# Five of 22 gate and value pairs of a gated MLP's up projection by seven quarter products, on one Trainium2 core

## Chip, cores and metric

One core of a Trainium2 chip runs the whole layer. The metric is device time in microseconds from the start to the end of one execution; lower is better. Engines are named as in the profile: PE (TensorE, with PEld for its weight loads), DVE (VectorE), ACT (ScalarE), POOL (GpSimd), and SP, whose queue issues most DMAs.

## What is computed

One layer of a streaming encoder on 512 tokens of width 1024, all in float32: parallel token mixers, cross attention into 256 memory tokens, and a gated MLP. The change is in the MLP, which is the last stage:

```python
hf = _rms_norm(x, norm_ffn_pre[l])
u = _dwconv_causal(hf @ w_up[l], ffn_dw[l]) + ffn_dw_b[l]      # w_up: 1024 x 5632, kernel of 3 taps
u_g, u_v = jnp.split(u, 2, axis=-1)                           # 2816 channels each
yff = (jax.nn.silu(u_g) * u_v) @ w_down[l]                    # w_down: 2816 x 1024
x = x + _rms_norm(yff, norm_ffn_post[l])
```

## The kernel before, in words

**Products of three terms.** A float32 matrix is held as a high part rounded to the type that PE multiplies fast, and a low part, the rest. `mm3` (L239) makes a product of three matmuls: high by high, high by low, low by high. `split` (L152) and `split_weights` (L179) make the two parts: an ACT cast for the high one, a DVE subtraction for the low one (L190 and L191 for weights, L1612 and L1613 in the last product).

**The order of work.** `run_blocks` (L203) takes jobs from a generator. Each job names a block of weights, which is loaded and split three jobs ahead, and a body that issues its matmuls. Split weights go into four tiles of each part, used in turn (`weights_tile`, L145). Raw weights come through two tiles `wr`, by SP's queue. From the program order a scheduler lays out each engine's queue when the program is built, by its own estimate of when things are ready. On the chip each engine then works through its queue in that fixed order. PSUM's eight banks are four tags of two (`sc`, `tr`, `mm`, `av`).

**The up projection** (`up_jobs`, L1550). 2816 channels are 22 blocks of 128. Pair j is the gate block and the value block of the same channels; its two jobs are n = 2j and 2j + 1. A job's product has 8 slices of the inner dimension by 3 terms: 24 matmuls of 512 tokens into one bank. `done` (L1553) turns the bank into the convolved channels: one ACT instruction (L1557), two DVE taps (`taps`, L590, recorded at L594). After the value job the gate is formed with a tanh (L1561) and two DVE operations (L1562, L1564). The result is the left half of a tile `qa` or `qb` of the pair of blocks. The first four jobs are done in two halves of 256 tokens, since the last tokens of `hf` come late.

**The last product** (`down_jobs`, L1599) is already made of seven products in place of eight: the 2x2 blocks are channel blocks and tokens on one side, channel blocks and output columns on the other. It needs sums of the activations, which POOL makes (`activation_sums`, L564, four operations of 256 columns for each two pairs), and sums of `w_down`, which the class `Sums` (L527) loads on ACT's queue, makes on DVE (L542 to L545) and stores to DRAM during the up projection. They come back as `dw` tiles, a ring of four buffers. The residual stays in SBUF in `ns.out` until the end (`finish`, L1704).

**Ends.** `norm_task` (L1290) gives `hf`, tile by tile of 128 tokens, and writes the residual into `ns.out`. `open_ffn` (L1538) frees the tiles of the attention and opens those of the MLP.

Of the kernel before, what the change touches and what calls it, by code (L numbers as in the profile page):

```python
# [17 lines left out]
F32 = mybir.dt.float32  # L18
# [20 lines left out]
HALF_SHIFT = 16  # L39
BIG = -float(2.0 ** 100)  # L40
# [43 lines left out]
def hybrid_layer(ctx: ExitStack, tc: tile.TileContext, a: dict, out: bass.AP):  # L84
# [146 lines left out]
    def matmul(ps, lhs, rhs, start, stop):  # L231
        PE.matmul(ps, lhs, rhs, start=start, stop=stop)  # L232
        bg.clock += max(int(math.prod(rhs.shape[1:])), 256) * 0.00042
# [293 lines left out]
    class Sums:  # L527


        def __init__(self, w, pairs, tile, queue, name):  # L530
            self.w, self.tile, self.queue, self.held = w, tile, queue, {}
            self.pairs, self.dram = pairs, dram.tile([pairs * P, 2 * D], F32, name=name)
# [7 lines left out]
        def add(self, q):  # L540
            (b11, b12), (b21, b22) = ((x[:, :S], x[:, S:]) for x in self.held[q])
            V.tensor_tensor(b22, b22, b12, ALU.subtract)  # L542
            V.tensor_tensor(b12, b12, b11, ALU.subtract)
            V.tensor_tensor(b11, b22, b11, ALU.add)
            V.tensor_tensor(b21, b21, b11, ALU.subtract)  # L545
# [762 lines left out]
    def open_mix_out():  # L1308
        close(m2)
        ns.res_, resp = new_pool("res", False)  # L1310
        ns.xr, ns.normed = None, []
        ns.out = [resp.tile([P, D], F32, name=f"res{t}") for t in range(NT)]
# [191 lines left out]
    def open_cross_out():  # L1504
# [5 lines left out]
        ns.hf = new_ht()  # L1510

# [26 lines left out]
    def open_ffn():  # L1538
        bg.drain("n1")
        close(ns.work_)  # L1540
        close(ns.xp_)
        close(ns.xm_)
        ns.fp_, ns.fp = new_pool("ffn", False)
        ns.work = ns.fp
        ns.quart = [(ns.fp.tile([P, 4, S // 2], F32, tag=f"qa{q}", name="qa"),
                     ns.fp.tile([P, 3, S // 2], F32, tag=f"qb{q}", name="qb")) for q in range(NF // 2)]
        ns.post = ns.fp.tile([P, D], F32, name="g_ffn")
        G.dma_start(ns.post, a["norm_ffn_post"][0].partition_broadcast(P))

    def up_jobs():  # L1550
        st, held = {}, []

        def done(j, i, ps):  # L1553
            if i == 0:
                st[j] = ns.fp.tile([P, 2, S], F32, tag="c", name="c", bufs=2)
            c, ch = st[j], i * NF + j
            st["first"] = A.activation(c[:, i], ps, AF.Identity, bias=pc("fb", ch), scale=pc("fdw2", ch)).ins  # L1557
            st["taps"] = taps(c[:, i], ps, lambda k: pc("fdw01", k * 44 + ch), 3).ins
            if i == 1:
                th = ns.fp.tile([P, S], F32, tag="th", name="th")  # L1560
                A.activation(th, c[:, 0], AF.Tanh, scale=0.5)  # L1561
                V.scalar_tensor_tensor(th, th, 1.0, c[:, 0], ALU.add, ALU.mult)  # L1562
                x = ns.quart[j // 2]
                V.scalar_tensor_tensor(x[j % 2][:, 0:2].rearrange("p a b -> p (a b)"), th, 0.5, c[:, 1],  # L1564
                                       ALU.mult, ALU.mult)
                if j % 2:
                    activation_sums(*x, G)


        for n in range(2 * NF):  # L1570
            def body(hi, lo, n=n):
                j, i = divmod(n, 2)
                if n > 3:
                    ps = bank()
                    channel_major(ps, (hi, lo), ns.hf)
                    done(j, i, ps)

                    q = n // 3 - 2
                    if 0 <= q < NF // 2:
                        with tc.issue_after(st["taps" if n % 3 == 0 else "first"]):  # L1580
                            (ns.sums.add, ns.sums.store, ns.sums.load)[n % 3](q + 2 * (n % 3 == 2))
                    return
                if n == 0:
                    bg.drain("n0")
                ps = bank(("mm", "sc")[n % 2])
                (channel_major if n else by_pass)(ps, (hi, lo), ns.hf, slice(0, S // 2))
                held.append((j, i, ps, (hi, lo)))
                if n == 3:
                    open_ffn()
                    for j, i, ps, w in held:  # L1590
                        (channel_major if i or j else by_pass)(ps, w, ns.hf, slice(S // 2, S))
                        done(j, i, ps)
                    ns.sums = Sums(w_down, NF // 2, lambda: ns.fp.tile([P, D], F32, tag="dw", name="wp", bufs=4), A,
                                   "sums")
                    ns.sums.load(0)
                    ns.sums.load(1)
            yield *cols(w_up, n % 2 * DFF + n // 2 * P), body, V, same, HALF_SHIFT if n < 4 else 0

    def down_jobs():  # L1599
# [4 lines left out]
        def load(n):  # L1604
            while len(raws) < min(n, 2 * len(order)):
                (phase, q), job = order[len(raws) // 2], len(raws) % 2
                raw = ns.fp.tile([P, D], F32, tag="dw", name="dw", bufs=4)
# [3 lines left out]
        def split_to(hi, lo, x):  # L1611
            A.copy(hi, x)  # L1612
            V.tensor_tensor(lo, x, hi.bitcast(F32), ALU.subtract)  # L1613

        def activations(phase, q):
# [13 lines left out]
            split_to(hi, lo, ns.quart[q][phase].rearrange("p a b -> p (a b)"))  # L1629
# [3 lines left out]
        def weights(phase, q, job):  # L1633
# [5 lines left out]
            if (phase, job) == (1, 1):  # L1639
                both = ns.fp.tile([P, D], F32R, tag=f"qa{q}", name="n4")  # L1640
# [3 lines left out]
            if (phase, q) == (1, pairs - 1):  # L1644
                hi, lo = (ns.fp.tile([P, D], F32R, tag="dw", name="dwr", bufs=4) for _ in range(2))
# [15 lines left out]
        def square(x, i, pieces=1):  # L1661
            n, ms = S // pieces, []
            for c in range(pieces):
                ms.append(ns.fp.tile([P, 1], F32, tag=f"pm{i}", name=f"pm{i}", bufs=4))
                A.activation(ns.fp.tile([P, S], F32, tag="th", name="junk")[:, :n], x[:, c * n:(c + 1) * n], AF.Square,
# [6 lines left out]
        def middle(job):  # L1672
# [11 lines left out]
            z7 = parts["z7"] = ns.fp.tile([P, 2, S], F32, name="z7")  # L1684
# [29 lines left out]
        def ends():  # L1714
# [23 lines left out]
            spare = [ns.fp.tile([P, D], F32, tag="dw", name="o", bufs=4) for _ in range(2)]  # L1738
# [81 lines left out]
```

## Time and profile before

| | |
|---|---|
| three runs | 1055.25, 1055.68 (median), 1055.97 us |
| the profiled execution | 1055.79 us, of which the profile spans 1054.0 us |
| first to last instruction of the MLP stage | about 696 to 1054 us of the span |
| mean granted clock of TensorE | 0.997 |

The profile shows one execution. Its page gives busy time by engine, slices of the span, the chain of work that ended last and the costliest groups of instructions; views of the trace give busy time by stage, groups by line and shape, single instructions in order of time, and waits. A PE instruction's own duration in these views is longer than the distance to the next one's start, since matmuls are pipelined: for PE's pace the starts count.

### The profile page before, as it was taken

To read this page: it belongs to the slowest core of one execution; us is meant where nothing else is said; L and a number is where in the kernel's file an instruction comes from. 1 tells how busy PE (TensorE), PEld (TensorE's weight loads), DVE (VectorE), ACT (ScalarE), POOL (GpSimd) and SP (SyncE) were. 2 spreads that over 40 slices of the span, in tenths; PEclk is the share of its full clock that TensorE was granted. 3 is DMA by queue.
4 is the path that set the end of the run, shared out by engine and by line. 5 is a ranking of instruction groups with operands and counts; after the bars stand their busy time and mean duration, and the time that the engine had idled before them with its cause. 6 is when DMAs were issued, how large, how long until landed. Compare 5 with 4: busy or idle time off the path is not lost.

```text
span 1054.0 us, 14559 instructions
## 1 busy us (share of the span) xinstructions
PE 1041.7 (99%) x5295; PEld 886.8 (84%) x5295; DVE 807.1 (77%) x1280; ACT 501.9 (48%) x823; POOL 184.3 (17%) x309
## 2 busy tenths in 40 slices
PE   9999999999999999999999999999999999999996
PEld 8888888888888988888888899998888888888885
DVE  6899997668667467867487798777878777777795
ACT  5322222277465365655444566554333333355661
POOL 4000000300231233433011031121112111111001
PEclk9999999999999999999999999999999999999998
DMA  8854434742342353232359644135576676626662
GB/s 276 282 168 102 103 100 142 193 109 81 116 140 82 100 161 101 80 100 85 96 172 284 207 132 126 60 111 190 186 243 229 214 233 215 196 81 211 210 188 80
DMA packets 165373, 163.08 MB, mean 155 GB/s; under 512 B 6527, under 2 KB 136172, under 8 KB 165045
## 3 DMA queue, kind: packets, MB, share of 16 engines
q1 hardware_dynamic: 152995, 119.91, 38.0%
q0 software_dynamic: 5824, 19.03, 6.2%
q10 hardware_dynamic: 6482, 23.21, 5.7%
q8 instruction: 42, 0.69, 0.3%
q14 instruction: 30, 0.25, 0.1%
HBM read 139.03 MB, written 23.09 MB: 154 GB/s over the span
## 4 chain that ended last, share of the span: by engine, by line
PE 99%; DVE 0%; ACT 0%; issue 0%; POOL 0%; POOLq 0%; DVEq 0%; ACTq 0%
PE ps_mm L232 51%; PE ps_av L232 31%; PE ps_sc L232 8%; PE ps_tr L232 4%; PE ps_tr L236 2%; PE ps_mm L442 1%; PE ps_av L442 1%; PE ps_mm L384 0%; PE ps_sc L389 0%; DVE o L1710 0%; PE ps_tr L426 0%; POOL st_m L270 0%; POOLq L1816 0%; ACT hth L155 0%; ACT hth L432 0%
## 5 line engine op out<-in xcount | busy, mean ns | idle before, releaser
L190 ACT CAST wh<-wr 128x1024 fp32r<-128x1024 f32 (+1 forms) x142 | 148.8, 1049 | 273.3 <-PE ps_mm L232 175.0
L191 DVE TENSOR_TENSOR wl<-wr,wh 128x1024 fp32r<-128x1024 f32 (+1 forms) x142 | 178.5, 1258 | 79.0 <-ACT wh L190 78.8
L232 PE MATMUL ps_mm<-hth,wh 128*128 128x512 f32 (+1 forms) x592 | 221.1, 380 | 0.2 <-ACT hth L155 0.2
L232 PE MATMUL ps_mm<-htl,wh 128*128 128x512 f32 (+1 forms) x592 | 220.7, 379 | 0.0
L232 PE MATMUL ps_mm<-hth,wl 128*128 128x512 f32 (+1 forms) x592 | 220.6, 379 | 0.0
L232 PE MATMUL ps_av<-htl,wh 128*128 128x512 f32 (+1 forms) x352 | 131.8, 374 | 0.0
L232 PE MATMUL ps_av<-hth,wh 128*128 128x512 f32 (+1 forms) x352 | 131.8, 374 | 0.0
L232 PE MATMUL ps_av<-hth,wl 128*128 128x512 f32 (+1 forms) x352 | 131.6, 374 | 0.0
L232 PEld LDWEIGHTS ps_mm<-hth,wh 128*128 128x128 f32 x592 | 109.6, 188 | 20.4 <-ACT hth L155 0.8
L232 PEld LDWEIGHTS ps_mm<-hth,wl 128*128 128x128 f32 x592 | 109.5, 188 | 20.1
L232 PEld LDWEIGHTS ps_mm<-htl,wh 128*128 128x128 f32 x592 | 109.6, 188 | 19.7
L665 DVE SCALAR_TENSOR_TENSOR y<-y,par,y 128x482 f32<-128x482 f32 (+29 forms) x120 | 83.3, 735 | 0.1
L232 PEld LDWEIGHTS ps_av<-hth,wl 128*128 128x128 f32 x352 | 66.1, 188 | 11.9
L232 PEld LDWEIGHTS ps_av<-hth,wh 128*128 128x128 f32 x352 | 66.2, 188 | 11.8
L232 PEld LDWEIGHTS ps_av<-htl,wh 128*128 128x128 f32 x352 | 66.0, 188 | 11.7
L1613 DVE TENSOR_TENSOR wl<-dw,wh 128x1024 fp32r<-128x1024 f32 x32 | 40.2, 1262 | 13.3 <-ACT wh L1612 13.1
L1612 ACT CAST wh<-dw 128x1024 fp32r<-128x1024 f32 x32 | 33.4, 1051 | 23.4 <-PE ps_tr L232 7.9
L1058 POOL TENSOR_SCALAR fbias<-ck,cq 128x128 f32<-128x128 f32 (+3 forms) x32 | 28.2, 888 | 63.0 <-DVE st L1065 59.7
L1561 ACT ACTIVATE th<-c 128x512 f32<-128x512 f32 x22 | 13.9, 632 | 48.0 <-DVE c L594 48.0
L155 ACT CAST pth<-ps_tr 128x512 fp32r<-128x512 f32 (+3 forms) x56 | 23.5, 448 | 24.7 <-PE ps_tr L236 24.6
L594 DVE SCALAR_TENSOR_TENSOR c<-ps_mm,par,c 128x510 f32<-128x510 f32 (+1 forms) x44 | 32.8, 744 | 0.7
L156 DVE TENSOR_TENSOR ptl<-ps_tr,pth 128x512 fp32r<-128x512 f32 (+3 forms) x56 | 27.5, 512 | 5.9 <-ACT pth L155 5.4
(493 smaller groups left out, 2132.5 us busy)
## 6 DMA issues: line engine op xcount, KB each, us to landing
wr<-in_w_up SPq DMA_DIRECT2D x44, 512.0 KB
wr<-in_w_in SPq DMA_DIRECT2D x38, 512.0 KB
wr<-in_w_gate SPq DMA_DIRECT2D x32, 512.0 KB
wp<-in_w_down ACTq DMA_DIRECT2D x22, 512.0 KB
sums<-wp ACTq DMA_DIRECT2D x22, 512.0 KB
dw<-sums SPq DMA_DIRECT2D x44, 256.0 KB
wr<-in_w_branch SPq DMA_DIRECT2D x16, 512.0 KB
wide<-in_w_out SPq DMA_DIRECT2D x12, 512.0 KB
```

Of the source, the lines that this page charges most:

```text
L155: A.copy(hi, ps)
L156: V.tensor_tensor(lo, ps, hi.bitcast(F32), ALU.subtract)
L190: order(A.copy(hi, raw[:, :n]))
L191: low.tensor_tensor(lo, raw[:, :n], hi.bitcast(F32), ALU.subtract)
L232: PE.matmul(ps, lhs, rhs, start=start, stop=stop)
L236: PE.transpose(ps, x, ident[:n, :n])
L442: keep(PE.matmul(banks[c][:, :S // 2], w[p == 1][:, k, c * P:(c + 1) * P], ht[p == 2][:, i * 4 + k, :S // 2], start=(i, p, k) == (0, 0, 0) ...
L594: ins = V.scalar_tensor_tensor(dst[:, s:], src[:, :S - s], w(k), dst[:, s:], ALU.mult, ALU.add)
L665: ins = V.scalar_tensor_tensor(dst[:, s:], src[:, :S - s], pc("conv_dw", k * 4 + j), dst[:, s:], ALU.mult, ALU.add)
L1058: G.tensor_scalar(bias[:, :w], ck[j][:, :w], -1.0, cq[:, qt, head:head + 1], ALU.mult, ALU.add)
L1612: A.copy(hi, x)
L1613: V.tensor_tensor(lo, x, hi.bitcast(F32), ALU.subtract)
```

## The change

Five pairs, j = 4, 7, 10, 13 and 16, are computed as 2x2 blocks in Winograd's form of Strassen's scheme. The blocks of the weights are gate and value by the two halves of the inner dimension (A11, A12, A21, A22), those of `hf` the halves of the inner dimension by two halves of the tokens. Seven products of 4 slices by 3 terms of 256 tokens take the place of the pair's 48 matmuls of 512 tokens.

- POOL forms four sums of `hf` once, behind the first four jobs (`token_terms`, eight operations of 1024 columns); ACT and DVE split them into the tiles that held the residual. For that, each finished residual tile is stored to a DRAM tensor `kept` on SP's queue in `norm_task`, and loaded again (`reload`) in the last product's second half.
- For each of the five pairs DVE forms four sums of the weights, 512 columns each. Three and a half weight tiles are split, not two. The raw weights come into the ring `dw`, which gets seven buffers.
- The five jobs of such a pair (three with seven products' weights, two of the next pair, done in the plain way between them) interleave, so that a bank read by ACT or DVE is not written at once again.
- Silu replaces tanh and one DVE operation, for all pairs.
- The sums of `w_down` take one step in a pair of seven products and its partner, two steps in a plain pair, and four in each of the last four pairs (j = 18 to 21). POOL's sums of the activations all move to these last four pairs, 44 operations as before. Splits of activations in the last product are made in two instructions, not one.

The diff, cut to its core:

```diff
+SEVEN_AT = (4, 7, 10, 13, 16)
...
@@ norm_task
+        else:
+            SP.dma_start(ns.kept[t * P:(t + 1) * P, :], ns.out[t])
...
+    def ring(dtype=F32, name="dw"):
+        return ns.fp.tile([P, D], dtype, tag="dw", name=name, bufs=7)
...
+    def token_terms():
+        tok = [slice(i * S // 2, (i + 1) * S // 2) for i in range(2)]
+        b = {}
+        for k, t in ((0, 0), (0, 1), (1, 1), (1, 0)):
+            ks = slice(4 * k, 4 * k + 4)
+            x = b[k, t] = ring(name="b").rearrange("p (k c) -> p k c", k=4)
+            G.tensor_tensor(x, ns.hf[0][:, ks, tok[t]].bitcast(F32), ns.hf[1][:, ks, tok[t]].bitcast(F32), ALU.add)
+            if (k, t) == (0, 1):
+                G.tensor_tensor(b[0, 0], x, b[0, 0], ALU.subtract)
...
+        for i, n in ((0, (0, 0)), (1, (1, 1)), (2, (0, 1)), (3, (1, 0))):
+            split(b[n], *ns.terms[i])
...
+        def gated(c, j):
+            A.activation(c[:, 0], c[:, 0], AF.Silu)
+            V.tensor_tensor(ns.quart[j // 2][:, j % 2 * 2:j % 2 * 2 + 2].rearrange("p a b -> p (a b)"), c[:, 0],
+                            c[:, 1], ALU.mult)
...
+        def quart_sums(n):
...
+            for q in range(len(ns.quart_sums), n):
...
+                G.tensor_tensor(two[:, 0], x[:, 1], x[:, 3], ALU.add)
+                G.tensor_tensor(two[:, 1], x[:, 0], x[:, 1], ALU.subtract)
+                G.tensor_tensor(x[:, 1], two[:, 0], x[:, 0], ALU.subtract)
+                G.tensor_tensor(one, x[:, 2], x[:, 1], ALU.subtract)
...
+            def product(ps, name, b, first=True):
+                hi, lo = w[name]
+                for k in range(4):
+                    for i, (w_p, x_p) in enumerate(((hi, b[0]), (hi, b[1]), (lo, b[0]))):
+                        matmul(ps[:, :S // 2], w_p[:, k], x_p[:, k], first and i == k == 0, i == 2 and k == 3,
+                               not first)
...
+            def first_weights():
...
+                weights(("A11", "A12"), g)
+                V.tensor_tensor(su[:, :S], v[:, :S], v[:, S:], ALU.add)
+                V.tensor_tensor(su[:, S:], su[:, :S], g[:, :S], ALU.subtract)
+                V.tensor_tensor(v[:, :S], g[:, :S], v[:, :S], ALU.subtract)
+                V.tensor_tensor(s4, g[:, S:], su[:, S:], ALU.subtract)
...
+            def first(_):
+                product(x["x"], "A11", old(0, 0))
+                A.copy(u[:, 0, 0], x["x"][:, :S // 2])
+                product(x["w"], "A12", old(1, 0))
+                add(u[:, 0, 0], x["w"])
+            def gate_first(hi, lo):
+                half_sums(*x["n"], range(4))
+            def second(_):
+                product(x["x"], "S2", ns.terms[1], False)
+                A.copy(kept["u"][:, 1, 0], x["x"][:, :S // 2])
+                step()
+            def third(_):
+                product(x["v"], "S3", ns.terms[2])
+                half_sums(*x["n"], range(4, NK))
+                done(n, 0, x["n"][0])
+                product(x["x"], "S1", ns.terms[0], False)
+                A.copy(u[:, 1, 1], x["x"][:, :S // 2])
+                add(u[:, 1, 1], x["v"])
+            def value(hi, lo):
+                half_sums(ps, (hi, lo), range(4))
+                product(x["x"], "S4", old(1, 1), False)
+                A.copy(u[:, 0, 1], x["x"][:, :S // 2])
+                half_sums(ps, (hi, lo), range(4, NK))
+                done(n, 1, ps)
+                product(x["v"], "A22", ns.terms[3], False)
+                add(u[:, 1, 0], x["v"])
...
+            yield first_weights, None, first
+            yield *plain(n, 0), gate_first, V, same, 0
+            yield second_weights, None, second
+            yield third_weights, None, third
+            yield *plain(n, 1), value, V, same, 0
...
+                        step(2 if j > seven[-1] + 1 else 1)
+                        if j > seven[-1] + 1:
+                            quart_sums(min(2 * (2 * (j - seven[-1] - 2) + i) + 2, (j + i) // 2))
...
+        def reload():
+            ns.out = [term_tile(t).rearrange("p a b -> p (a b)") for t in range(NT)]
+            for t in range(NT):
+                SP.dma_start(ns.out[t], ns.kept[t * P:(t + 1) * P, :])
...
-            split_to(hi, lo, ns.quart[q][phase].rearrange("p a b -> p (a b)"))
+            split_to(hi[:, :S], lo[:, :S], flat(ns.quart[q][:, 2 * phase:2 * phase + 2]))
+            split_to(hi[:, S:], lo[:, S:], new)
...
+            if (phase, q, job) == (1, 2, 0):
+                reload()
```

More of the change, by code (lines that the diff above doesn't have):

```diff
@@ L1510, in open_cross_out @@
         ns.hf = new_ht()
+        ns.kept = dram.tile([S, D], F32, name="kept")
     def cross_out_jobs():
@@ L1570, in up_jobs @@
[L1570 to L1591, printed above, removed]
-                        done(j, i, ps)
[L1593 to L1597, printed above, removed]
@@ new lines, in done, with sums, step @@
+                gated(st[j], j)
+        def sums():
+            ns.sums = Sums(w_down, NF // 2, lambda: ring(name="wp"), A, "sums")
+            for q in range(NF // 2):
+                yield ns.sums.load, q
+                yield ns.sums.add, q
+                yield ns.sums.store, q
+        steps = sums()
+        def step(n=1):
+            for _ in range(n):
+                f, q = next(steps, (None, None))
+                if f is not None:
+                    with tc.issue_after(st["taps" if f == ns.sums.add else "first"]):
+                        f(q)
@@ L1599, in down_jobs @@
+        j = 0
+        while j < NF:
+            yield from (seven_jobs if j in seven else plain_jobs)(j)
+            j += 2 if j in seven else 1
+        for f, q in steps:
+            yield then(lambda f=f, q=q: f(q))
     def down_jobs():
@@ L1644, in weights @@
             if (phase, q) == (1, pairs - 1):
-                hi, lo = (ns.fp.tile([P, D], F32R, tag="dw", name="dwr", bufs=4) for _ in range(2))
+                hi, lo = (ring(F32R, "dwr") for _ in range(2))
             else:
@@ L1736, in whole @@
                 return x
-            spare = [ns.fp.tile([P, D], F32, tag="dw", name="o", bufs=4) for _ in range(2)]
+            spare = [ring(name="o") for _ in range(2)]
             spare.append(gp.tile([P, WB], F32, tag="wr", name="wr", bufs=2)[:, :D])
```

135 lines of the change are left out of this document (110 added, 25 removed).

## The prediction

> **What bounds the kernel now.** I read the page first: the busy times of the engines and the chain that ended last.
>
> ```profile
> span 1054.0 us, 14559 instructions
> PE 1041.7 (99%) x5295; PEld 886.8 (84%) x5295; DVE 807.1 (77%) x1280; ACT 501.9 (48%) x823; POOL 184.3 (17%) x309
> PE 99%; DVE 0%; ACT 0%; issue 0%; POOL 0%; POOLq 0%; DVEq 0%; ACTq 0%
> ```
>
> PE is the chain from end to end. Next, the busy time by stage: the up projection behind its first blocks, the stretch around its end, and a stretch of the last product. The columns after the stretch are its length, then PE, PEld, DVE, ACT and POOL busy, the granted clock, the DMA engines' share and GB/s.
>
> ```profile
> 722.00:960.00 238.00, 238.00 (x1051) 196.93 (x1050) 185.29 (x224) 96.28 (x116) 41.88 (x44) 1.00 0.61 197
> 941.00:963.00 22.00, 22.00 (x98) 18.13 (x97) 18.46 (x17) 13.71 (x15) 3.08 (x3) 1.00 0.54 168
> 985.00:1007.00 22.00, 22.00 (x98) 18.21 (x97) 18.52 (x23) 14.91 (x20) 0.00 (x0) 1.00 0.70 210
> ```
>
> PE never rests at a full clock, and DVE is the next busiest: 185.29 of 238 us, 78%. So a matmul column saved in the up projection is time saved, as long as DVE, which the change loads further, keeps its distance. That distance is the next thing to read, in the chain in order of time (start, length, what) and in DVE's instructions one by one (start, length).
>
> ```profile
> 612.22 5.65 PE ps_mm L232 x48
> ...
> 731.80 5.44 PE ps_mm L232 x24
> ...
> 753.56 5.44 PE ps_mm L232 x24
> ```
>
> ```profile
> 738.13 1.23 DVE L191 TENSOR_TENSOR wl<-wr,wh 128x1024 fp32r<-128x1024 f32 x1 [1.55 <-ACT wh L190]
> ```
>
> A block is 24 matmuls of 512 columns, 5.44 us. The low part at 738.13 is the 11th in the up projection, that of job 10, whose matmuls start at 753.56: it is ready 753.56 - 739.36 = 14.2 us early. Nothing that makes DVE less than that late reaches PE in the middle of the stage.
>
> **The matmuls, which are the gain.** A plain pair is 48 matmuls of 512 columns, 2 x 5.44 = 10.88 us. A pair of seven products is 7 x 4 x 3 = 84 matmuls of 256 columns. The 48 at 612.22 have that width and follow 512 wide ones: 5.65 / 48 = 0.1177 us each. They do not cost half of 0.2267 but 0.0044 more. 84 x 0.1177 = 9.89, so 0.99 us less a pair, 4.97 for five. Another stretch is faster:
>
> ```profile
> 698.59 1.25 PE ps_sc L232 x11
> ```
>
> 1.25 / 11 = 0.1136 us; 84 of these are 9.54 us, which would make it 6.7 us for five pairs. I take 0.1177, since the 48 at 612.22 follow wide matmuls, as here, and keep the other for the range. Going back from 256 to 512 columns isn't free either:
>
> ```profile
> 720.73 0.40 PE L232 MATMUL ps_av<-hth,wh 128*128 128x512 f32 x1
> ...
> 722.12 0.39 PE L232 MATMUL ps_mm<-htl,wh 128*128 128x512 f32 x1
> ```
>
> Six wide matmuls take 1.39 us there, 0.03 over 6 x 0.2267. A pair with its partner makes this change five times (before both halves of the gate block, both of the value block, and the next pair), 25 times in all: 0.7 us back. **Gain on PE: 4.97 - 0.7 = 4.3 us.**
>
> By the Trainium skill, "TensorE: Matmul & The Clock Gate", Back-to-back issue gap, a warm matmul takes its columns at 2.4 GHz and about 2.5 ns more, 215.8 and 109.2 ns for 512 and 256; estimated from that page the five pairs would save 5.9 us. The rows here are slower, 226.7 and 117.7 ns, and the sum goes by them.
>
> **What the change adds on DVE and ACT.** The groups by shape between 744 and 918 us (count, busy us, mean ns, idle before):
>
> ```profile
> L191 DVE TENSOR_TENSOR wl<-wr,wh 128x1024 fp32r<-128x1024 f32 x33 | 42.7, 1294 | 27.9 <-ACT wh L190 27.9
> L594 DVE SCALAR_TENSOR_TENSOR c<-ps_mm,par,c 128x511 f32<-128x511 f32 x16 | 12.0, 750 | 0.6
> L1562 DVE SCALAR_TENSOR_TENSOR th<-th,c 128x512 f32<-128x512 f32 x16 | 11.0, 690 | 8.3 <-ACT th L1561 8.3
> L544 DVE TENSOR_TENSOR wp<-wp 128x512 f32<-128x512 f32 x10 | 9.0, 900 | 0.2
> L545 DVE TENSOR_TENSOR wp<-wp 128x512 f32<-128x512 f32 x11 | 8.6, 781 | 0.0
> L542 DVE TENSOR_TENSOR wp<-wp 128x512 f32<-128x512 f32 x10 | 6.8, 681 | 0.0
> L190 ACT CAST wh<-wr 128x1024 fp32r<-128x1024 f32 x32 | 33.5, 1048 | 68.3 <-PE ps_mm L232 54.0 <-PE ps_av L232 9.2 <-DMA wr<-in_w_up 5.2
> L1557 ACT ACTIVATE c<-ps_mm,par 128x512 f32<-128x512 f32 x16 | 12.3, 771 | 0.0
> ```
>
> Three pairs, one of them of seven products, are PE's 2 x 10.88 + 9.89 = 31.65 us. DVE has in them 7 low parts by 1.29 and one of half width by 0.69; four sums of weights by 0.69; 12 taps by 0.75; three gate products by 0.69; one group of `w_down` sums, four by 0.69; and three sums of a bank of 256 columns by 0.42 (row below). Together 27.6 us, 87%. The same count for three plain pairs before (6 low parts, 12 taps, 6 gate operations, 2 groups of sums) is 26.4 of 32.6, 81%, where the stage shows 78%. DVE stays under PE; the cover is 4.1 us in three pairs, and were it gone, each further us of DVE would be one of the total.
>
> ```profile
> L1731 DVE TENSOR_TENSOR o<-o,ps_av 128x256 f32<-128x256 f32 x1 | 0.4, 420 | 0.1
> L155 ACT CAST xqh<-ps_mm 128x256 fp32r<-128x256 f32 x4 | 1.5, 366 | 2.2 <-PE ps_mm L232 2.2
> L1070 ACT ACT_TABLE_LOAD x1 | 1.3, 1283 | 0.5 <-DVE st L1068 0.5
> ```
>
> ACT has 7 casts by 1.05, one half, six instructions by 0.77, three Silu and four bank copies by 0.37: some 16 of 31.65 us. Silu needs a function table, one load of 1.28 us, or two a pair if the table holds no Identity (2.6 of 10.88 us): ACT has room for both. I take nothing.
>
> **Added waits.** S2, S1 and S4 add to a bank that ACT has just copied, A22 to one that DVE has just read. Between the read and the write lie 12 or more matmuls: A12 and half the gate block ahead of S2 (1.41 + 2.72 us), S3 and the other half ahead of S1 (4.1), half the value block ahead of S4 (2.72). A copy is 0.37 us, so nothing, if it isn't queued behind something longer; that is a rival below.
>
> **POOL and the port that it shares.** DVE and POOL in order of time:
>
> ```profile
> 791.04 1.12 POOL L566 TENSOR_TENSOR qa<-qa,qb 128x256 f32<-128x256 f32 x1 [10.02 <-DVE qb L1564]
> ...
> 791.60 1.11 DVE L544 TENSOR_TENSOR wp<-wp 128x512 f32<-128x512 f32 x1
> ...
> 792.24 1.07 POOL L568 TENSOR_TENSOR qa<-qa 128x256 f32<-128x256 f32 x1
> ...
> 792.63 1.76 DVE L191 TENSOR_TENSOR wl<-wr,wh 128x1024 fp32r<-128x1024 f32 x1
> ```
>
> L544 takes 1.11 us beside POOL, where L542 alone has a mean of 0.68; L191 1.76 against 1.23. So each meeting of two such operations costs DVE about 0.5 us. The Trainium skill has a rule for it, "SBUF — State Buffer", Who interferes with whom: a DVE instruction with two SBUF inputs and a POOL instruction that reads SBUF exclude each other for the whole instruction. These rows agree.
>
> In the last four pairs 44 POOL operations stand in 8 blocks, 43.5 us, where before they were spread over 20 pairs. DVE's own work per block there is 1.23 + 2 x 0.75 + 0.35 + 2.5 sums x 0.69 = 4.8 of 5.44 us, with four operations that can meet POOL. The groups between 744 and 918 us have this line for POOL, and three more with a count of 8:
>
> ```profile
> L567 POOL TENSOR_TENSOR qa<-qa 128x256 f32<-128x256 f32 x8 | 7.0, 874 | 64.0 <-DVE qa L1564 64.0
> ```
>
> By DVE's means there (L544 0.22, L545 0.10, L191 0.06 us over their undisturbed lengths, 10, 11 and 33 times) these 32 POOL operations cost DVE 5.4 us, 0.17 each: 44 are 7.4 us, 0.9 a block, and DVE ends 8 x (4.8 + 0.9 - 5.44) = 2 us late. If each of the four meets POOL it is 2.0 a block, and 11 us late. At the boundary the cover is thinner than inside:
>
> ```profile
> 946.42 1.21 DVE L1613 TENSOR_TENSOR wl<-dw,wh 128x1024 fp32r<-128x1024 f32 x1
> ```
> ```profile
> 950.31 0.39 PE L232 MATMUL ps_sc<-wl,hth 128*128 128x512 f32 x1
> ```
>
> 2.7 us from the end of a low part to the first matmul that reads it. I take 2 us late and no loss; the other end is a loss of 8 us.
>
> The sums of `hf` are eight POOL operations of 1024 columns. The widest row is 512:
>
> ```profile
> L415 POOL TENSOR_TENSOR wa<-e,wa 128x512 fp32r<-128x512 f32 x4 | 5.1, 1297 | 1.8 <-ACT wa L412 1.8
> ```
>
> From 256 columns (0.87) to 512 it is 0.43 more, so 1024 are between 1.30 + 2 x 0.43 = 2.2 and 2 x 1.30 = 2.6 us, and eight some 20 us. They wait for `hf`, whose last part DVE writes here, ahead of the first low part for the blocks behind it:
>
> ```profile
> 709.30 1.29 DVE L156 TENSOR_TENSOR htl<-ps_tr,hth 128x512 fp32r<-128x512 f32 x2 [2.71 <-ACT hth L155]
> 714.71 1.23 DVE L191 TENSOR_TENSOR wl<-wr,wh 128x1024 fp32r<-128x1024 f32 x1 [4.12 <-ACT wh L190]
> ```
>
> So POOL is done about 731, later where DVE is ahead of it. The first split sum is read by S2 of pair 4, at 731.80 + 2 x 5.44 + 2.8 + 2.7 = 748.2. DVE loses up to 2.6 us at each meeting, and there may be five; the low part at 714.71 has 4.8 us until its matmuls at 720.73, later ones more. I take nothing, and 0 to 4 us for the range.
>
> **DMAs.** Four stores of residual tiles, 2 MB, go into SP's queue; each waits for DVE's residual, and the weight loads behind it wait too, with the lead of a low part as cover. The gain vector's load moves on POOL's queue to the last four pairs, ahead of the 44 sums; nothing reads it before the last product's middle. The four loads of `reload` are 2 MB more on SP's queue in a stage at 210 GB/s and 0.70 of the DMA engines, 300 GB/s at full share: 7 us in which the weights behind them wait, with seven buffers in the ring, not four, as cover, which are two or three blocks more. I take nothing; without that cover it would be up to 7 us.
>
> The last product's splits in two pieces cost DVE 2 x 0.69 - 1.29 = 0.09 us each and ACT as little, beside a PE that is full. **Sum:** 1055.79 - 4.3 = 1051.5 for an execution like the profiled one; the median of the runs is 0.11 lower, so **1051.4 us.**
>
> **Rivals.**
> *Narrow matmuls at half price* (0.1136 us, as at 698.59): 6.7 - 0.7, so 1049.7. Against it: the longest narrow row with wide ones ahead has 0.1177.
> *DVE late from POOL.* For it: DVE at 84% in 941 to 963 and a cover of 2.7 us. It gives 1 to 8 us back, 1052.4 to 1059, most likely near 1055; the sums of `hf` would do the same at the stage's start.
> *A copy behind a cast,* the one that ends slower. ACT's queue is in order, and its casts of weights wait for PE to leave a tile: 54.0 of 68.3 us of idle before L190. In a pair of seven the gate block's tile is held until its second half, so the cast that takes it waits until just before S1. If the copy ahead of S1 stands behind that cast in ACT's queue, PE waits for 1.05 + 0.37 us and the hand-overs, about 1.8 us a place. With one such place a pair the five give 9 us: 1060. Three places (5.4 us) take more than the gain, four (7.2) make it slower by more than a measurement of this kernel can blur, 0.2% or 2.1 us.
> *Nothing gained:* narrow matmuls would have to cost 10.88 / 84 = 0.1295 us; no row has that.
>
> **How the numbers follow.** Forecast 0.47 (1050.4 to 1052.4), half price 0.08, DVE late 0.23, copy behind a cast 0.19, nothing gained 0.03. Faster by over 0.2%: the first two, and 0.07 of DVE late, 0.62. Within: 0.10 of DVE late, 0.02 of the copies (up to three places), and nothing gained, 0.15. Slower: 0.06 and 0.17, 0.23. The range runs from 1049.5, half price, to 1059, the worst of DVE late; it leaves out the copies from four places on.
>
> **What would show it.** Right: PE without gaps from 722 to the last block, five stretches of 84 narrow matmuls with starts 0.118 us apart, the last product's start 4 us earlier. DVE late: gaps ahead of matmuls that read a low part, around 935 to 955 or 720 to 750, with DVE rows lengthened beside POOL. Copies: gaps ahead of S1 or S4, ended by ACT. The prediction is wrong if PE rests in the pairs of seven, or the starts lie further apart than 0.12 us.

## The result, and the profile after

The changed kernel takes 1064.66 us (median of 4 runs, 1063.56 to 1066.92) where the kernel before takes 1055.62 in the same comparison: a ratio of 1.0089, 95% interval 1.0071 to 1.0106. The forecast was 1051.4, its range 1049.5 to 1059. The profiled execution, 1066.92 us, spans 1065.1. The page's totals and the line of its chain:

```profile
span 1065.1 us, 15055 instructions
PE 1042.2 (98%) x5475; PEld 893.2 (84%) x5475; DVE 830.0 (78%) x1329; ACT 523.0 (49%) x880; POOL 208.4 (20%) x317
PE 85%; DVE 8%; DMA 3%; issue 2%; ACT 1%; POOL 0%; DVEq 0%; POOLq 0%; ACTq 0%; SPq 0%
```

PE's busy time is that of before (1041.7), and the span is 11 us longer: PE waits, and DVE and DMAs have entered the chain. To find where, I take four PE rows of each trace, in order of time (start, own length, what): the first matmul behind the last part of `hf`, the first of the last product, and the last listed group. Before, then after:

```profile
709.32 0.38 PE L232 MATMUL ps_mm<-hth,wh 128*128 128x256 f32 x1 [0.24 <-ACT hth L155]
...
938.36 0.39 PE L232 MATMUL ps_sc<-wh,wr 128*128 128x512 f32 x1
...
1043.06 0.52 PE L232 MATMUL ps_av<-dwr,a 128*128 128x256 f32 x3
```
```profile
711.63 0.39 PE L233 MATMUL ps_mm<-hth,wh 128*128 128x256 f32 x1 [0.24 <-ACT hth L156]
...
937.63 0.40 PE L233 MATMUL ps_sc<-wh,wr 128*128 128x512 f32 x1
...
1053.85 0.52 PE L233 MATMUL ps_av<-dwr,a 128*128 128x256 f32 x3
```

The up projection took 229.04 us and takes 226.00: **3.0 less.** The last product took 104.70 and takes 116.22: **11.5 more.** The up projection starts 2.3 later, and 0.3 more stands at the end; together 11.1, the spans' difference. (Over the kernels below, which share the code up to there, that start lies between 709.7 and 711.8, so most of the 2.3 is scatter between executions.)

**The pairs of seven work as forecast.** Two stretches of the fourth pair of seven, from the chain:

```profile
847.20 2.83 PE ps_sc L233 x24
...
850.02 2.75 PE ps_mm L233 x12
```

24 narrow matmuls in 2.83 us are 0.118 each. From 778.10 to 809.86, at which points the order of products repeats, three pairs with one of seven take 31.76 us, 0.88 less than three plain ones (3 x 10.88); five times that is 4.4. The up projection holds one gap, in the first pair of seven, where S1 (one of the seven products, named in the diff) waits for its low part:

```profile
751.52 0.28 PE L233 MATMUL ps_sc<-t,wh 128*128 128x256 f32 x1
753.33 0.38 PE L233 MATMUL ps_sc<-t,wl 128*128 128x256 f32 x1 [1.53 <-DVE wl L192]
```

That is 1.81 where 0.12 was due, 1.7 lost; without it the stage is 4.7 us shorter.

**The loss is at the boundary.** PE's gaps in the last product's first blocks:

```profile
943.59 0.40 PE L233 MATMUL ps_av<-wh,wr 128*128 128x512 f32 x1
947.03 0.50 PE L233 MATMUL ps_sc<-wh,hth 128*128 128x512 f32 x1 [3.04 <-ACT hth L1787]
...
953.32 0.39 PE L233 MATMUL ps_av<-wh,hth 128*128 128x512 f32 x1
956.93 0.80 PE L233 MATMUL ps_sc<-wl,hth 128*128 128x512 f32 x1 [3.22 <-DVE wl L1788]
...
958.81 0.63 PE L233 MATMUL ps_tr<-wl,hth 128*128 128x512 f32 x1
959.23 0.63 PE L233 MATMUL ps_tr<-wh,hth 128*128 128x512 f32 x1
```

Two waits of over 3 us, for an activation's cast and for a low part; and behind the second the starts lie 0.43 us apart instead of 0.227, for 12 matmuls: 2.4 us more. Smaller waits of 1.05 and 0.43 us stand ahead of 942.34 and 950.92; all of these together are most of the 11.5. What ACT and DVE did instead, in order of time. ACTq is ACT's queue busy with issuing a DMA or waiting to; a bracket is the idle time before a row and what ended it.

```profile
925.44 2.07 ACTq L550 DMA_DIRECT2D sums<-wp  x2
927.56 0.78 ACT L1586 ACTIVATE c<-ps_mm,par 128x512 f32<-128x512 f32 x1 [4.07 <-DVE wp L546]
...
940.79 2.45 ACTq L539 DMA_DIRECT2D wp<-in_w_down  x2
943.33 0.63 ACT L1590 ACTIVATE c<-c 128x512 f32<-128x512 f32 x1 [3.74 <-DMA sums<-wp]
...
944.80 0.61 ACT L1787 CAST htl<-qa 128x512 fp32r<-128x512 f32 x1
```
```profile
923.27 0.69 DVE L543 TENSOR_TENSOR wp<-wp 128x512 f32<-128x512 f32 x1 [2.12 <-DMA sums<-wp]
...
945.43 0.69 DVE L543 TENSOR_TENSOR wp<-wp 128x512 f32<-128x512 f32 x1 [3.23 <-DMA wp<-in_w_down]
946.04 1.22 DVE L1788 TENSOR_TENSOR wl<-dw,wh 128x1024 fp32r<-128x1024 f32 x1
...
955.65 1.23 DVE L1788 TENSOR_TENSOR wl<-dw,wh 128x1024 fp32r<-128x1024 f32 x1
```

What the queues wait for in these rows is `Sums`. A group's load (L539) waits in ACT's queue until an earlier group's store has left a buffer; its add (L543) waits in DVE's queue until the load has landed; its store (L550) waits in ACT's queue for the add. Behind each stand the casts and low parts that the last product needs at once. The low part at 955.65 ended PE's second long wait. By then DVE waited for nothing: from 945.43 on it worked without a rest, six of Sums' late adds of 0.69 us among the work ahead of that low part. So late loads and late adds both have a part in it. The DMA engines are nearly full around the boundary. Stretches by their length, then PE, PEld, DVE, ACT, POOL, granted clock, DMA share, GB/s; before, then after:

```profile
919.00:941.00 22.00, 22.00 (x99) 18.16 (x98) 15.04 (x18) 9.11 (x11) 3.81 (x4) 1.00 0.23 73
963.00:985.00 22.00, 22.00 (x98) 18.21 (x97) 15.23 (x14) 12.03 (x13) 0.00 (x0) 1.00 0.64 197
```
```profile
919.00:941.00 22.00, 22.00 (x98) 18.03 (x96) 19.57 (x27) 9.09 (x12) 3.85 (x4) 1.00 0.94 321
941.00:963.00 22.00, 14.26 (x48) 10.36 (x47) 17.95 (x26) 9.64 (x15) 2.63 (x4) 0.84 0.83 283
963.00:985.00 22.00, 22.00 (x99) 18.22 (x98) 15.24 (x17) 13.61 (x18) 0.62 (x1) 1.00 1.01 367
```

Before, Sums were done ahead of 919, with 73 GB/s left; now the engines are at 0.94 and 1.01 on both sides of the stall, and at 0.83 in it.

### The profile page after: what moved, and what is told of

It reads as the page before. It is cut to its first block, busy times and chain, and to the rows that moved or that the text cites. A ratio compares the mean times of both kernels' runs of the same rounds, so it can differ in the third digit from the quotient of the medians.

```text
span 1065.1 us, 15055 instructions
## 1 busy us (share of the span) xinstructions
PE 1042.2 (98%) x5475; PEld 893.2 (84%) x5475; DVE 830.0 (78%) x1329; ACT 523.0 (49%) x880; POOL 208.4 (20%) x317
## 4 chain that ended last, share of the span: by engine, by line
PE 85%; DVE 8%; DMA 3%; issue 2%; ACT 1%; POOL 0%; DVEq 0%; POOLq 0%; ACTq 0%; SPq 0%
PE ps_mm L233 43%; PE ps_av L233 23%; PE ps_sc L233 11%; PE ps_tr L233 4%; DVE wl L192 2%; PE ps_tr L237 2%; DVE c L595 1%; DMA wp<-in_w_down 1%; DMA wr<-in_w_up 1%; DMA mix<-in_w_xkv 1%; ACT wh L191 1%; DVE qa L1591 1%; PE ps_mm L443 1%; PE ps_av L443 1%; DVE wl L1788 0%
## 5 line engine op out<-in xcount | busy, mean ns | idle before, releaser
L191 ACT CAST wh<-wr 128x1024 fp32r<-128x1024 f32 (+1 forms) x132 | 138.3, 1049 | 228.6 <-PE ps_mm L233 129.6
L192 DVE TENSOR_TENSOR wl<-wr,wh 128x1024 fp32r<-128x1024 f32 (+1 forms) x132 | 170.6, 1294 | 71.7 <-ACT wh L191 71.1
L233 PE MATMUL ps_mm<-hth,wh 128*128 128x512 f32 (+1 forms) x552 | 205.8, 380 | 0.2 <-ACT hth L156 0.2
L233 PE MATMUL ps_mm<-htl,wh 128*128 128x512 f32 (+1 forms) x552 | 205.4, 379 | 0.4 <-DVE htl L157 0.4
L233 PE MATMUL ps_mm<-hth,wl 128*128 128x512 f32 (+1 forms) x552 | 205.0, 378 | 0.0
L233 PE MATMUL ps_av<-hth,wh 128*128 128x512 f32 (+1 forms) x312 | 116.3, 373 | 0.0
L233 PE MATMUL ps_av<-htl,wh 128*128 128x512 f32 (+1 forms) x312 | 116.3, 373 | 0.0
L233 PE MATMUL ps_av<-hth,wl 128*128 128x512 f32 (+1 forms) x312 | 116.1, 372 | 0.0
L1632 POOL TENSOR_TENSOR t<-qa 128x256 f32<-128x256 f32 x10 | 8.8, 882 | 161.1 <-PE ps_sc L233 148.1
L1590 ACT ACTIVATE c<-c 128x512 f32<-128x512 f32 x22 | 13.9, 632 | 47.3 <-DVE c L595 43.5
```

Source lines behind the costliest of these rows:

```text
L191: order(A.copy(hi, raw[:, :n]))
L192: low.tensor_tensor(lo, raw[:, :n], hi.bitcast(F32), ALU.subtract)
L233: PE.matmul(ps, lhs, rhs, start=start, stop=stop, skip_group_check=more)
L1590: A.activation(c[:, 0], c[:, 0], AF.Silu)
```

## Experiments

Theory 1: the 16 of Sums' 33 steps that stand in the last four pairs make the stall. Theory 2: POOL's 44 sums do. Each time is a median, the ratio against the kernel before on the same chip, with its interval; to compare experiments I take ratios, since "before" differs by up to 0.6 us between chips. Line numbers shift by a few between kernels.

**1. Sums spread.** A pair of seven and its partner takes three steps, a plain job one.

```diff
@@ third, behind done(n, 0, ...), and value, behind done(n, 1, ps)
+                step()
@@ plain_jobs
-                        step(2 if j > seven[-1] + 1 else 1)
+                        step(1)
```

> The steps of Sums (load, add, store of w_down's 11 groups) go three to each pair of seven products instead of one, and one to each plain product at the stage's end instead of two, so that 6 of 33 steps instead of 16 stand in the last four pairs. Theory 1 (the Sums crammed into the last pairs hold ACT's queue and DVE back at the boundary; TensorE idle 940-960 of 10.4 us, and about 2 us of lower clock behind it): the stall goes, 1051 to 1055 us, with no gap of over 1 us on TensorE between the two products. Theory 2 (GpSimd's 44 sums, which stay where they are, make VectorE late): 1063 to 1066. If the ring of seven buffers makes the earlier loads wait instead, a new gap stands in the middle of the stage, 1056 to 1062.

1055.5 us, 0.9994 (0.9985 to 1.0003): 10 us come back. PE's waits at the boundary have shrunk to one:

```profile
941.90 0.40 PE L233 MATMUL ps_av<-wh,wr 128*128 128x512 f32 x1
...
943.37 0.51 PE L233 MATMUL ps_sc<-wh,hth 128*128 128x512 f32 x1 [1.07 <-ACT hth L1789]
```

Theory 1 holds for most, but the time is just above its 1055, and only that of before.

**2. No pair of seven, Sums spread; 3. no pair of seven, Sums crammed.** In both `SEVEN_AT = ()`; in the second 17 steps stand ahead of the last four pairs and 16 in them.

```diff
-SEVEN_AT = (4, 7, 10, 13, 16)
+SEVEN_AT = ()
@@ plain_jobs, run 2, and run 3
+                        step(1)
+                        step(2 if j > 17 else 1 if i == 0 or j == 17 else 0)
```

> No pair by seven products (all 22 plain); all else of the change stays: token terms, gate by Silu, residual kept and loaded again, splits in two pieces, GpSimd's 44 sums in the last four pairs. With no pairs of seven, Sums go one step to each plain product, done before the last four pairs. Theory 1: no stall at the boundary but no gain either, the time of before plus the 1 to 2.5 us that the stage's start loses: 1056 to 1058. Theory 2: 1063 to 1068, as the stall stays and the gain of 4.3 is given up.

> No pair by seven products as in the run without them, but Sums crammed as in the changed kernel: 17 of 33 steps before the last four pairs, 16 in them. If the cramming alone makes the stall (theory 1), this kernel, which has no other part of the seven products left, has the gap on TensorE at the boundary of the two products again: 1064 to 1070 us, 8 to 13 more than the 1056.6 without the cramming. If it takes the seven products as well (their narrower lead or VectorE's load), 1056 to 1059.

1056.63, 1.0006 (0.9996 to 1.0015), against 1063.56, 1.0064 (1.0050 to 1.0078). So all of the change but the seven products costs nothing measurable (`kept`, `reload`, Silu, the splits in two pieces), and cramming alone costs 6.1 us, a little less than expected, with the later of the two long waits; the earlier one, for an activation's cast, is not there. DVE and PE of run 3:

```profile
942.16 0.69 DVE L543 TENSOR_TENSOR wp<-wp 128x512 f32<-128x512 f32 x1 [2.73 <-DMA wp<-in_w_down]
```
```profile
953.66 0.79 PE L233 MATMUL ps_sc<-wl,hth 128*128 128x512 f32 x1 [3.19 <-DVE wl L1787]
```

**4. Sums of groups 6 to 10 left out,** POOL's sums kept.

```diff
-            for q in range(NF // 2):
+            for q in range(6):
@@ Sums.parts
-self.dram[q * P:(q + 1) * P, ...]
+self.dram[q % 6 * P:(q % 6 + 1) * P, ...]
```

> The Sums of groups 6 to 10 are left out (loads, adds and stores; the last product loads the sums of groups 0 to 4 again in their place, same bytes), so that the last four pairs have almost none. Theory 1: 1051 to 1054, VectorE and ACT's queue without waits for w_down before the boundary. Theory 2: 1062 to 1065.

Six of ten runs lie at 1053.7 to 1055.7, four at 1065.1 to 1067.4; median 1054.86, 1.0026 (0.9989 to 1.0064). In the profiled run, 1053.87, the boundary has no gap. The four I could not explain then; run 16 takes them up.

**5. The changed kernel without POOL's 44 sums; 6. the same with Sums spread.**

```diff
-                G.tensor_tensor(two[:, 0], x[:, 1], x[:, 3], ALU.add)
...
-                ns.quart_sums[q] = two, one
+                ns.quart_sums[q] = x[:, 2:4], x[:, 1]
```

> GpSimd's 44 sums for the last product are left out (the second half of each split reads the gated values themselves, so the last product's operands are wrong); splits, Sums and seven products stay. Theory 1: the boundary's stall stays, 1061 to 1065. Theory 2: it goes, 1051 to 1055.

> As the kernel with Sums spread, but GpSimd's 44 sums of the last pairs are left out (so the last product's operands are wrong). With Sums out of the way this prices GpSimd's meeting with VectorE by itself. If they hold VectorE on the path (theory 2 as a second cause): the gap of 1.2 us at the boundary goes and the time is 1052.5 to 1054. If VectorE has room there: 1055 to 1056, with the gap still there.

1060.47, 1.0048 (1.0033 to 1.0063), and 1053.62, 0.9980 (0.9971 to 0.9989). So POOL is a second cause: 4.3 us where Sums are crammed, 1.5 where they are spread, and there the last gap at the boundary goes. Theory 1's and theory 2's numbers for run 5 were both missed, theory 1's by 0.5 us; in its profiled execution the boundary's waits stay, of 2.56 and 3.21 us.

**7. Sums' DMAs from POOL's queue.**

```diff
-ns.sums = Sums(w_down, NF // 2, lambda: ring(name="wp"), A, "sums")
+ns.sums = Sums(w_down, NF // 2, lambda: ring(name="wp"), G, "sums")
```

> The changed kernel with the Sums' loads and stores issued from GpSimd's queue instead of ACT's; adds stay on VectorE. If what counts is ACT's queue, held by a store that waits for VectorE's last add or by a load that waits for a buffer (theory 1a): the stall mostly goes, 1053 to 1057. If VectorE's own wait for the landing of a group's load is enough (theory 1b): 1060 to 1066, and a new wait may come as the loads stand behind GpSimd's sums.

1066.38, 1.0080 (1.0060 to 1.0100): nothing gained. DVE still waits for a landing:

```profile
951.93 0.69 DVE L543 TENSOR_TENSOR wp<-wp 128x512 f32<-128x512 f32 x1 [3.83 <-DMA wp<-in_w_down]
```

Taking the DMAs out of ACT's queue does not end the stall. What share that queue has in the changed kernel stays open, as new waits came on POOL.

**8. Sums spread, token sums left out; 9. Sums spread, pairs of seven at 5, 8, 11, 14, 17.** Both aim at the gap at 751. What stands behind it in the changed kernel's trace, DVE and POOL:

```profile
725.20 2.20 DVE L192 TENSOR_TENSOR wl<-wr,wh 128x1024 fp32r<-128x1024 f32 x1 [0.35 <-ACT wh L191]
727.33 2.90 DVE L1591 TENSOR_TENSOR qa<-c 128x512 f32<-128x512 f32 x1
...
730.81 2.76 DVE L192 TENSOR_TENSOR wl<-wr,wh 128x1024 fp32r<-128x1024 f32 x1
```
```profile
723.91 2.41 POOL L1572 TENSOR_TENSOR b<-b 128x1024 f32<-128x1024 f32 x1
726.40 3.28 POOL L1573 TENSOR_TENSOR b<-b 128x1024 f32<-128x1024 f32 x1
729.75 2.73 POOL L1575 TENSOR_TENSOR b<-b 128x1024 f32<-128x1024 f32 x1
```

Three DVE operations of 1.2, 0.7 and 1.2 us elsewhere take 2.2, 2.9 and 2.8 beside POOL: 4.8 us. A fourth, the low part at 718.80, takes 2.77 beside the first of POOL's sums: 1.5 us more.

```diff
@@ token_terms, run 8 (the POOL sums above it are gone)
-            split(b[n], *ns.terms[i])
+            split(ns.hf[0][:, 4 * n[0]:4 * n[0] + 4, tok[n[1]]].bitcast(F32), *ns.terms[i])
@@ run 9
+SEVEN_AT = (5, 8, 11, 14, 17)
```

> As the kernel with Sums spread, but GpSimd's eight token sums are left out (the four term tiles are split from the normalised activations themselves, so five pairs' operands are wrong). If these sums, running beside VectorE at 720 to 733, make it late (its 1024-wide low parts 2.2 to 2.8 us there instead of 1.2): VectorE's operations there take their usual time and the 1.7 us gap in the first pair of seven goes: 1053 to 1054.2. If VectorE is full there from its own additions: 1055 to 1056.

> Sums spread three steps to a pair of seven, and the five pairs of seven one pair later (5, 8, 11, 14, 17 instead of 4 to 16), so that VectorE has a plain pair more to come back from GpSimd's token sums. If the 1.7 us gap in the first pair of seven is VectorE's lateness from the stage's start: it goes, and the time is 1052 to 1054. If the quarter products' operands come late for a reason of that pair alone, the gap moves along: 1055 to 1057; three plain pairs instead of four at the end may bring a gap of 1 to 3 us at the boundary back: 1055 to 1058.

Run 8: 1053.61, 0.9972 (0.9962 to 0.9982), 2.3 us under run 1 by the ratios; the low parts and the gate product are back at 1.2 and 0.7, and the gap is gone. Run 9: 1056.01, 1.0001 (0.9992 to 1.0010). The gap is gone there too, but with three plain pairs at the end one of 2.0 us is back at the boundary.

**10. Sums four steps to a pair of seven** (one more, in `gate_first`)**; 11. with the pairs at 5, 8, 11, 13, 16.**

```diff
@@ gate_first
                 half_sums(*x["n"], range(4))
+                step()
@@ run 11
+SEVEN_AT = (5, 8, 11, 13, 16)
```

> Sums four steps to a pair of seven (one more, behind the plain companion's first half) and one to each plain product, so that they end before the last four pairs; pairs of seven where the changed kernel has them. If the last group, added by VectorE at 929 to 933 in the kernel with three steps, holds the activation casts: the gap of 1.2 us at the boundary goes, 1053.5 to 1055. If the ring of seven buffers can't carry more: a gap of over 1 us in the middle of the stage, 1056 or more.

> Sums four steps to a pair of seven, and the pairs of seven at 5, 8, 11, 13, 16 instead of 4, 7, 10, 13, 16: one plain pair more behind GpSimd's token sums, still four plain pairs at the end, and no plain pair between 12 and 13. If the two gaps (first pair of seven 1.7 us, boundary 1.2 us) are VectorE's lateness from the stage's start and from the last Sums: both go, and the gain of the seven products is left, 1051.5 to 1053.5. If VectorE can't carry two pairs of seven in a row: a gap at pair 13, 1054 to 1057.

1062.74, 1.0071 (1.0055 to 1.0086), and 1063.7, 1.0075 (1.0062 to 1.0087). The boundary has no gap now, but the last pair of seven has one that I had put down to the ring. It isn't the ring. PE, DVE and POOL of run 10:

```profile
898.73 0.58 PE L233 MATMUL ps_sc<-t,wh 128*128 128x256 f32 x1 [6.67 <-DVE u L1671]
```
```profile
886.40 11.94 DVE L192 TENSOR_TENSOR wl<-wr,wh 128x1024 fp32r<-128x1024 f32 x1
```
```profile
886.90 2.13 POOL L1634 TENSOR_TENSOR qa<-t,qa 128x256 f32<-128x256 f32 x3
...
894.50 2.75 POOL L1634 TENSOR_TENSOR qa<-t,qa 128x256 f32<-128x256 f32 x4
```

One low part lasts 11.94 us, from 886.40 to 898.34, while POOL runs sums without a break until 897.25: it is done 1.1 us after POOL falls idle, its usual length.

**12. Run 10 with the 44 sums on DVE; 13. run 11 likewise; 14. run 11 with every second group's on DVE; 15. run 13 with three steps to a pair of seven.**

```diff
-                G.tensor_tensor(two[:, 0], x[:, 1], x[:, 3], ALU.add)
+                V.tensor_tensor(two[:, 0], x[:, 1], x[:, 3], ALU.add)
...
```

> As the kernel with Sums four steps to a pair of seven (1062.7), but the 44 sums for the last product run on VectorE instead of GpSimd. If GpSimd's unbroken run held VectorE's low part for 11.9 us: the 6.8 us gap at 892 goes and nothing but the 1.4 us gap in the first pair of seven is left, 1052.5 to 1054.5. If VectorE's own load or the ring made that gap: it stays or grows with 17 us more of VectorE's work, 1062 to 1068.

> As the one above, with the pairs of seven at 5, 8, 11, 13, 16. If the three losses (Sums, GpSimd's sums, VectorE's lateness in the first pair) are all there is: TensorE has no gap of over 0.6 us from the first product's start to the end of the last, and the forecast gain of 4.3 us is left less 0.5 to 1 at the start, 1051.5 to 1053. If VectorE is the bound in the last four pairs with 17 us more: a gap of 1 to 5 us at the boundary, 1053 to 1057.

> As the one above, but only every second group's sums on VectorE, the others on GpSimd. If it takes a long unbroken run of GpSimd to hold VectorE: 1051.5 to 1053.5. If half of the run holds it half as long: one VectorE operation of 5 to 7 us near 885 and a gap of 1 to 4 us, 1053 to 1057.

> Sums three steps to a pair of seven (6 of 33 steps in the last four pairs), pairs of seven at 5, 8, 11, 13, 16, and the 44 sums on VectorE. If VectorE can carry both in the last four pairs: 1051.5 to 1053. If not, a gap at the boundary of 1 to 4 us that the kernel with four steps doesn't have: 1053 to 1057.

Run 12: 1053.48, 0.9975 (0.9966 to 0.9984). The gap at 892 is gone, so POOL made it. Run 13: 1053.47, 0.9976 (0.9965 to 0.9987), half a microsecond above what I expected; its largest gap is 0.5 us. Run 14: 1057.38, 1.0011 (1.0002 to 1.0020), with a gap of 2.6 us at 892.6: no single operation is held long (2.4 us at most), but many are doubled. Run 15: **1052.92, 0.9968 (0.9955 to 0.9980), the lowest median of those that compute all,** and clear of both kernels' times; its interval overlaps those of runs 12 and 13. Its PE rows:

```profile
709.81 0.39 PE L233 MATMUL ps_mm<-hth,wh 128*128 128x256 f32 x1 [0.24 <-ACT hth L156]
...
934.57 0.39 PE L233 MATMUL ps_sc<-wh,wr 128*128 128x512 f32 x1
...
1039.28 0.52 PE L233 MATMUL ps_av<-dwr,a 128*128 128x256 f32 x3
```

The up projection takes 224.76, 4.28 less than before, and the last product 104.71, as before.

**16. Run 4 with the 44 sums on DVE; 17. the changed kernel with them on DVE, nothing else.** The edit is that of run 12.

> As the kernel without the Sums of groups 6 to 10 (the last product loads the sums of groups 0 to 4 in their place), and the 44 sums for the last product on VectorE instead of GpSimd. If GpSimd's run of sums makes the executions at 1065 to 1067: none is left, all at 1052.5 to 1055. If they come from somewhere else: about four of ten are at 1063 or more again.

> The changed kernel with the 44 sums on VectorE instead of GpSimd, Sums crammed as they are. If the crammed Sums are the larger part and GpSimd the smaller: 1058 to 1062, with gaps of 6 to 9 us at the boundary. If GpSimd is what makes VectorE late there: 1052 to 1055. If VectorE can't carry both: 1064 to 1070.

Run 16: all ten runs at 1053.45 to 1055.57, none long where run 4 had four of ten, so its four long ones most likely needed POOL's sums; that they were held as in run 10 is a guess, since none of the four was traced. Run 17: 1061.2, 1.0039 (1.0026 to 1.0052). Against run 12, its twin with Sums spread, cramming alone costs 6.8 us. With POOL idle there DVE waits less, but the loads of the sums themselves come late; ACT's row:

```profile
951.91 1.06 ACT L1787 CAST wh<-dw 128x1024 fp32r<-128x1024 f32 x1 [6.46 <-DMA dw<-sums]
```

**The ledger, by ratios.** The changed kernel and runs 1, 5 and 6 are the four corners of a square: Sums crammed or spread three steps to a pair, POOL's sums there or left out. From the changed kernel to run 6, with both causes gone, it is 11.5 us. Crammed Sums alone are 7.2 of it (runs 5, 6), POOL's sums alone 1.5 (runs 1, 6), and some 2.8 arise only where both meet. The 1.5 holds for that pace of Sums: with four steps to a pair of seven, taking the sums off POOL is worth 10.1 (runs 10, 12). And the 7.2 is the price of the moved steps as a whole: no run takes away their adds alone or their DMAs alone.

## Why the prediction was wrong, step by step

**The gain, 4.3 us: right.** Narrow matmuls cost 0.118 us, not half of 0.2267, and run 15's up projection is 4.28 us shorter, with a gap of some 0.5 in it. Half price is refuted; so is that nothing was gained. My reason for taking 0.1177 was weak, though: right ahead of the 48 matmuls at 612.22 stand 26 narrow ones (609.15), not wide ones. The changed kernel has the pace right behind wide ones too, 12 in 1.42 us at 853.22. Why the row at 698.59 is faster stays open.

**DVE and ACT carry the additions: right** in the middle of the stage. No gap stands between 760 and 935, and in runs 11 and 13 not even where two pairs of seven follow each other.

**Added waits, and the rival of a copy behind a cast: nothing, right.** In the changed kernel no gap stands ahead of a product that waits for a bank's copy. (Run 7 has one of 1.44 us, ahead of 784.47: the copy there stood behind an ACT instruction that had itself waited 2.9 us for DVE.) Slower came, but not by the mechanism that I had mainly put on that side. The other one, DVE late from POOL, fits the place, since a low part ended the second long wait; but its mark is missing: the low parts at 946.04 and 955.65 take 1.22 and 1.23 us, undisturbed.

**Sums of `hf`, taken as nothing, range 0 to 4: a term mis-sized.** They end at 732.5, where I had 731, and cost DVE 6.3 us in four meetings. The lead of the first low parts covered PE for a while, but DVE (the third busy time) could not come back, full with its own additions:

```profile
722.00:744.00 22.00, 22.00 (x102) 18.32 (x102) 21.65 (x21) 13.18 (x15) 10.25 (x4) 1.00 0.47 148
744.00:766.00 22.00, 20.47 (x125) 18.18 (x124) 21.99 (x33) 8.91 (x13) 0.00 (x0) 1.00 0.79 236
```

So 1.7 us were lost at S1. PE resting in a pair of seven was one of my signs of being wrong.

**POOL in the last four pairs, "2 us late and no loss": mis-sized.** 0.17 us an operation came from a stage in which POOL rested between groups. In long runs the 44 cost 1.5 to 4.3 us (runs 1 and 6, the changed kernel and run 5), and 10.1 in run 10, where one DVE operation stood for 10.7 us. So my forecast of no loss was too low, and for run 10 so was the far end of 8 us.

**The step that failed is DMAs, "I take nothing".** There I priced the kept residual and its reload, which cost nothing that run 2 can show, and counted Sums' steps only as DVE's 2.5 x 0.69 us a block. That the moved steps bring their loads and stores, and a wait in two in-order queues for each, I left out: a term put at nothing. The runs put 7.2 us on the moved steps alone, and 10.0 where POOL's sums run too (run 1 against the changed kernel). The bytes could have been worked out:

```profile
wp<-in_w_down ACTq DMA_DIRECT2D x22, 512.0 KB
sums<-wp ACTq DMA_DIRECT2D x22, 512.0 KB
```

A group is two loads and two stores of 512 KB, 2.1 MB. 16 steps are 5.3 groups, 11.2 MB; over the last four pairs' 43.5 us that is 257 GB/s, and the weights' eight loads of 512 KB are 96 more: 353, against the 300 at full share on which I had priced the reload (the changed kernel's trace has up to 367, at 1.01). The steps did not keep up: from 894.00 to 937.60 the trace has 251 GB/s at a share of 0.77, and the last two groups' first adds come at 945.43 and 950.78, behind the boundary. With the three steps of a group in two in-order queues, each late landing holds casts and low parts. How much of the loss is late landings, how much the queues' order and how much the late adds stays open. A high share by itself does not make the stall: in run 15 the engines stand at 0.90, 0.78 and 0.86 in three stretches of 22 us from 897 on, and PE has no gap there. I had also taken 2.7 us as the cover at the boundary and let POOL alone use it up.

**The clock** was in no step: after the wait of 3.2 us it cost 2.4 us more.

## What to carry to other kernels

When steps of a side job are moved together, divide all bytes of their DMAs by the time of the new place, and follow each step's waits through every in-order queue that it stands in; here I had counted only its arithmetic (20 adds of 0.69 us, 14 us of DVE), not its 11.2 MB. Work moved to another engine to relieve DVE must be priced where it runs back to back, not where it rests between pieces. And where a good gain is in place (4.3 us here), look first for what was moved to make room for it: pacing Sums anew, with POOL's sums on DVE and the pairs of seven shifted, gave 1052.9 with the same products.

## What the runs showed of the hardware

**One DVE operation can stand until a whole unbroken run of POOL has ended.** In run 10 a low part of 1.2 us lasted 11.94 beside 15 POOL operations of 0.7 us without a break, and in run 11 14.48. The Trainium skill, "SBUF — State Buffer", Who interferes with whom, has an exclusive lock that whoever starts first holds for a whole instruction. By that alone the wait would end with one POOL operation, 0.7 us; the measurement is 15 times that. In the changed kernel the same two queues took turns (its low parts there 1.8 us). What decides between the two is open.

**A wait of a few us can halve the clock, and its length alone does not tell when.** Behind the wait of 3.22 us ahead of 956.93 the starts lie 0.427 us apart, 12 times, where 0.227 is the pace; the mean granted clock of 941 to 963 is 0.84. The Trainium skill, "TensorE: Matmul & The Clock Gate", Part 1, states half the clock after an idle window of about 3.4 us; this wait, with starts 3.61 us apart, agrees, but others do not sort by length. Behind waits of 3.04 (ahead of 947.03), 2.56 (run 5) and 1.07 us (run 1) the pace stayed. In run 14, behind one of 2.59 us ahead of 895.55, the starts soon lie 0.43 us apart too, with a granted clock of 0.52 from 896.5 to 898.5, and in run 17 behind one of 2.05 us ahead of 962.48, with 0.65 from 965 to 968. What decides is open.
